# Differential attention scores as three 64-row products per component instead of two stacked 128-row products

## The chip, the cores and the metric

The kernel runs on one core of one Trainium2 chip. The metric is the device time of one launch in microseconds (us), lower is better. A core has TensorE (PE, the matrix products, with weight loads shown as PEld), VectorE (DVE), ScalarE (ACT), GpSimd (POOL) and SyncE (SP, which here only issues transfers). PE reads its operands from SBUF, 128 partitions of on-chip memory, and writes its results to PSUM.

## The reference

The network is an encoder of two layers on 512 tokens with 1024 channels. Each layer projects the normalised input and mixes tokens in three parallel branches (differential attention, a convolution module, neighbourhood attention on an 8 x 64 grid), merges them by gates, and then runs a gated feed-forward part and a gated embedding. The change touches the differential attention alone. It has four heads; each head has two components `c` of 64 channels:

```python
q = apply_rope(q, cos, sin)
k = apply_rope(k, cos, sin)
...
s = jnp.einsum('bhcqd,bhckd->bhcqk', qi, k).astype(f32) * scale
a = jax.nn.softmax(s, axis=-1)
a = (a[:, :, 0] - lam * a[:, :, 1]).astype(v.dtype)
return jnp.einsum('bhqk,bhkd->bhqd', a, v)
```

So for each head and each block of 128 queries there are two score matrices of 128 x 512, each a product over 64 channels; two softmaxes; their difference; and a product with the values. All of it is in float32.

## The kernel before

**Products in halves.** PE multiplies the type float32r, which keeps fewer bits than float32. To keep float32 accuracy each operand is split into a high half (rounded to float32r) and a low half (the rest, again float32r): `split` (L162) makes the high half by an ACT copy and the low half by a DVE subtraction. A general product then is three products into one PSUM tile: high by high, high by low, low by high (`mm3`, L175). The low-by-low term is left out there.

**Order of the work.** The program is written out layer by layer in `layer` (L428). The order of PE's instructions is the order in which the program issues them; the other engines are ordered by a scheduler that follows their dependencies and priorities. While PE works through the projections of one branch, pieces of attention are put in between: `later` (L107) puts a generator in a queue, and every fourth group of three products (`chunk`, L115) one `tick` (L94) may start or go on with one. Each differential head queues four `diff_unit`s (L844), one per block of 128 queries, two ticks apart. A unit runs `probs` (L892), which makes the scores and the softmax difference; every second unit goes on three ticks later with eight transposes (L859) for its pair of blocks and two ticks after that with the product with the values.

**Queries and keys of a head.** `diff_in` (L813) projects queries and keys of one head, each 128 rows (two components of 64) by 512 tokens. It copies the projection out of PSUM into `raw`, makes a rotated copy `rot` with four small transfers (L829), applies the position tables on DVE, and splits the result into `nat` (high, tile tag `kh`) and `low` (in place in `raw`). Then `stack` (L654) copies these halves by transfers of 64 partitions on SP's queue into a layout with one component per column block and the halves above each other: in `st4` (tag `qk`, two buffers) rows 0 to 63 hold a component's high half and rows 64 to 127 its low half; in `k2` (tag `x`, four buffers) the keys stand the other way round, low above high. That is four transfers for the queries and eight for the keys of each head (L660).

**Scores.** `scores` (L807) contracts over all 128 rows at once. The first product, stacked queries by stacked keys, gives high by high plus low by low; the second, stacked queries by the swapped keys, gives high by low plus low by high. So one component costs two products of 128 rows by 512 columns, and both components of a block four. `probs` takes a PSUM tile (tag `sc`, two buffers) for a component, makes its scores, then its maximum on DVE (L902) and its exponential on ACT (L143, a helper's line), and goes on to the other component. The neighbourhood attention uses `stack` and `scores` as well, with its own tiles.

**Who shares the buffers.** The tag `x` also holds the gate accumulators of `gate_c` (L762), which ACT copies out of PSUM. The tags `rp` (four buffers), `kh` (two) and `qk` (two) are also used by other stages.

Of the kernel before, what the change touches and what calls it, by code (L numbers as in the profile page):

```python
# [12 lines left out]
F32R = mybir.dt.float32r  # L13
# [7 lines left out]
P = 128  # L21
# [40 lines left out]
class Net:  # L62
# [744 lines left out]
    def scores(self, out, st4, k2, u, qs, ks):  # L807


        for n, st in enumerate((st4[:, 2 + u], k2[:, u])):  # L810
            self.nc.tensor.matmul(out, st4[:, u, qs], st[:, ks], start=n == 0, stop=n == 1)  # L811

    def diff_in(self, head, st, ys):  # L813
        self.phase = "diff"
        if head == 0:
            st["tabs"] = []
            for t in range(2):
                c = self.sb("r", [P, 512])
                self.nc.sync.dma_start(c, self.a["rope"][t])
                st["tabs"].append(c)  # L820
        st4 = self.sb("qk", [P, 4, 512], F32R)
        k2 = self.sb("x", [P, 2, 512], F32R)
        for s, off in enumerate((OFF_QA, OFF_KA)):
            ps = self.proj(off + head * P)
            raw, rot = self.sb("rp", [P, 512]), self.sb("rp", [P, 512])
            self.act(raw, ps, AF.Copy, scale=1.0 if s else 0.125)
            for b in range(4):
                o = b ^ 1
                self.nc.sync.dma_start(rot[32 * b:32 * b + 32], raw[32 * o:32 * o + 32])  # L829
            self.background(self.tt(raw, raw, st["tabs"][0], ALU.mult), self.bg["diff"])  # L830
            self.tt(rot, rot, st["tabs"][1], ALU.mult)
            self.tt(raw, raw, rot, ALU.add)
            nat, low = self.sb("kh", [P, 512], F32R), raw.bitcast(F32R)
            self.split(nat, low, raw)
            self.stack(nat, low, st4[:, 2 * s:2 * s + 2], k2 if s else None)
        box = dict(s0=self.sb("sm", [P, 4]))
        for qt in range(4):
            self.later(self.diff_unit(head, qt, st4, k2, st, box, ys), 6 if head else 7, 2)

    def diff_v(self, g, st):  # L840
        self.phase = "diff"
        st["v", g] = self.values(self.a["w_va"][self.i, g], lambda v, a: ((v[:, 0:256], v[:, 256:512], a),))

    def diff_unit(self, head, qt, st4, k2, st, box, ys):  # L844

        nc, i = self.nc, self.i
        half, t = qt // 2, qt % 2
        box[qt] = self.probs(st4, k2, qt, box["s0"])
        if t == 0:
            return  # L850
        yield 3
        ats = [box[2 * half], box[2 * half + 1]]
        pps = []
        for kp in range(2):
            pt = self.ps("tr", (P, 2, 256))
            for u in range(2):
                for t in range(2):
                    kc = 2 * kp + u
                    nc.tensor.transpose(pt[:, u, t * P:(t + 1) * P],  # L859
                                        ats[t][:, kc * P:(kc + 1) * P], self.ident)  # L860
            pp = self.sb("pt", [P, 2, 2, 256], F32R)
            self.split(pp[:, 0], pp[:, 1], pt)
            pps.append(pp)
        yield 2
        if half == 0:
            box["av"] = self.ps("av")
        av = box["av"]
        cs = slice((head % 2) * P, (head % 2) * P + P)
        for kp in range(2):
            for u in range(2):  # L870
                v = st["v", head // 2][kp][:, u].rearrange("p (a b) -> p a b", a=2)
                self.mm3(av[:, half * 256:half * 256 + 256], v[:, 0, cs], v[:, 1, cs],
                         pps[kp][:, 0, u], pps[kp][:, 1, u], kp * 2 + u == 0, kp * 2 + u == 3)
        if half == 0:
            return

        eps = self.sb("sm", [P, 4])
        self.stt(eps, box["s0"], EPS, box["s0"], ALU.mult, ALU.mult)
        o = self.sb("t", [P, 512])
        sq = self.sb("ss", [P, 512])  # L880
        self.act(sq, av, AF.Square)
        self.act(o, av, AF.Copy, scale=self.subg[:, i:i + 1])

        def done(col, bc):
            self.tt(o, o, bc, ALU.mult)
            y = self.sb("y", [P, 2, 512], F32R)
            self.split(y[:, 0, :], y[:, 1, :], o)
            ys.append(y)

        yield from self.norm(sq, P, (1, 2), done, spread=False, eps=eps)  # L890

    def probs(self, st4, k2, qt, s0):  # L892


        nc, i = self.nc, self.i
        qs = slice(qt * P, (qt + 1) * P)
        m = self.sb("s", [P, 10])
        es = []
        for u in range(2):
            sc = self.ps("sc")  # L900
            self.scores(sc, st4, k2, u, qs, slice(0, 512))
            nc.vector.tensor_reduce(out=m[:, u:u + 1], in_=sc, op=ALU.max, axis=AX.X, negate=True)  # L902
            e = self.sb("e" if u else "a", [P, 512])
            self.act(e, sc, AF.Exp, table="exp", bias=m[:, u:u + 1],
                     accum_out=m[:, 3:4] if u else s0[:, qt:qt + 1])
            es.append(e)
        nc.vector.reciprocal(m[:, 4:5], m[:, 3:4])
        self.stt(m[:, 5:6], m[:, 4:5], self.nlam[:, i:i + 1], s0[:, qt:qt + 1],
                 ALU.mult, ALU.mult)
        self.stt(es[0], es[1], m[:, 5:6], es[0], ALU.mult, ALU.add)  # L910
        return es[0]
# [555 lines left out]
```

## Time and profile before

| what | us |
|---|---|
| time, median of 3 runs | 1776.03 |
| lowest and highest run | 1776.01, 1777.37 |
| span of the profiled execution, first to last instruction | 1776.7 |
| PE busy in it | 1767.5 |
| DVE busy | 1421.7 |
| ACT busy | 894.4 |

The profiled execution's own device time is not listed apart from its span; the span lies inside the range of the runs. In the profile's lines L12 is line 12 of the kernel, and a tile is named by the stage in which it was made and its tag: `diff_qk` is the stacked tile of the differential attention, `diff_x` its `k2`, `diff_sc` its scores. `out<-in` names what is written and read, `x16` is a count. A duration of PE is that of one product from its start to its modelled end; products are pipelined, so the distance of two starts, and not the duration, is what one costs in a row of them. A view of waits gives the total in us, how many times, and the longest. A form such as `128*128 128x512` gives first the rows and columns of the array that a product is set for, then the size of the result.

### The profile page before, as it was taken

What the parts mean: (1) busy time and instruction counts of PE and PEld (TensorE: products, weight loads), DVE (VectorE), ACT (ScalarE), POOL (GpSimd) and SP (SyncE); (2) the same over time, 40 slices, a digit from 0 to 9 for tenths busy, and PEclk for the clock granted to TensorE, in tenths of its full rate; (3) what the DMA queues carried; (4) which work ended last, traced back from release to release, by engine and by line L of the source; (5) the groups of instructions that cost most, each with busy time, mean ns of one, the idle gap of its engine ahead of it and who ended that gap; (6) DMA issues with size and microseconds to landing.
All of it is one profiled execution on the core that took longest, in us unless ns stands there. A gap on an engine that the chain in (4) does not pass through costs nothing.

```text
span 1776.7 us, 27451 instructions
## 1 busy us (share of the span) xinstructions
PE 1767.5 (99%) x10210; PEld 1559.6 (88%) x10210; DVE 1421.7 (80%) x2418; ACT 894.4 (50%) x1561; POOL 103.0 (6%) x146
## 2 busy tenths in 40 slices
PE   9999999999999999999999999999999999999998
PEld 7888888888899899998888888888888998989987
DVE  7878887998798587787776788889887976867776
ACT  5577555225565254454545765452356643534454
POOL 0000000000111010100000000000001110101000
PEclk9999999999999999999999999999999999999999
DMA  5666641334757366543447655423357664655332
GB/s 202 188 186 176 161 125 42 113 98 140 230 150 193 109 167 160 132 131 123 145 124 198 176 165 149 113 71 95 93 179 198 171 179 115 173 144 151 98 108 92
DMA packets 113509, 256.07 MB, mean 144 GB/s; under 512 B 14560, under 2 KB 19424, under 8 KB 113376
## 3 DMA queue, kind: packets, MB, share of 16 engines
q1 hardware_dynamic: 99984, 229.93, 42.3%
q0 software_dynamic: 12672, 23.07, 8.3%
q8 instruction: 81, 1.33, 0.3%
q10 hardware_dynamic: 720, 1.31, 0.2%
q14 instruction: 52, 0.43, 0.1%
HBM read 215.46 MB, written 7.34 MB: 125 GB/s over the span
## 4 chain that ended last, share of the span: by engine, by line
PE 96%; DVE 2%; ACT 1%; issue 0%; DMA 0%; POOL 0%; ACTq 0%; POOLq 0%; DVEq 0%
PE ffn_mm L1017 4%; PE ffn_mm L1019 4%; PE ffn_mm L177 4%; PE ffn_mm L179 4%; PE ffn_mm L178 4%; PE ffn_mm L1018 4%; PE ffn_sc L1019 3%; PE ffn_sc L1017 3%; PE ffn_sc L1018 3%; PE mergea_mm L177 2%; PE mergea_mm L178 2%; PE mergea_mm L179 2%; PE diff_sc L811 2%; PE gatec_mm L177 2%; PE gatec_mm L178 2%; PE gatec_mm L179 2%
## 5 line engine op out<-in xcount | busy, mean ns | idle before, releaser
L160 DVE SCALAR_TENSOR_TENSOR conv_z<-glu_z,pre_par,conv_z 128x512 f32<-128x512 f32 x240 | 179.4, 748 | 3.3
L143 ACT ACTIVATE ffn_wh<-ffn_wr 128x1024 fp32r<-128x1024 f32 (+1 forms) x92 | 92.7, 1014 | 111.7 <-PE ffn_mm L178 77.1
L987 POOL DMA_DIRECT2D ffn_qk<-w_fu x88 | 78.0, 990 | 605.7 <-DMA ffn_qk<-w_fu 414.7
L157 DVE TENSOR_TENSOR ffn_wl<-ffn_wr,ffn_wh 128x1024 fp32r<-128x1024 f32 (+1 forms) x92 | 107.4, 1173 | 5.4 <-ACT ffn_wh L143 4.9
L157 DVE TENSOR_TENSOR ffn_t<-ffn_mm,wo_rb 128x512 f32<-128x512 f32 (+1 forms) x64 | 38.6, 604 | 67.9 <-PE ffn_mm L179 67.8
L143 ACT ACTIVATE mergea_wh<-mergea_wr 128x1024 fp32r<-128x1024 f32 (+1 forms) x32 | 27.1, 846 | 96.8 <-PE mergea_mm L178 79.6
L143 ACT ACTIVATE ffn_wh<-ffn_qk 128x1024 fp32r<-128x1024 f32 x44 | 46.7, 1060 | 35.9 <-PE ffn_mm L178 15.7
L157 DVE TENSOR_TENSOR ffn_wl<-ffn_qk,ffn_wh 128x1024 fp32r<-128x1024 f32 x44 | 53.8, 1224 | 11.3 <-ACT ffn_wh L143 11.3
L157 DVE TENSOR_TENSOR ffn_t<-ffn_t,ffn_t 128x512 f32<-128x512 f32 (+1 forms) x46 | 31.3, 680 | 31.4 <-ACT ffn_t L143 30.9
L143 ACT ACTIVATE diff_a<-diff_sc,diff_s 128x512 f32<-128x512 f32 x32 | 22.0, 686 | 61.0 <-DVE diff_s L902 61.0
L177 PE MATMUL ffn_mm<-ffn_v,ffn_wh 128*128 128x512 f32 x132 | 51.4, 389 | 0.0
L178 PE MATMUL ffn_mm<-ffn_v,ffn_wh 128*128 128x512 f32 x132 | 51.4, 389 | 0.0
L179 PE MATMUL ffn_mm<-ffn_v,ffn_wl 128*128 128x512 f32 x132 | 51.3, 389 | 0.0
L177 PE MATMUL ffn_mm<-ffn_y,ffn_wh 128*128 128x512 f32 x132 | 51.3, 389 | 0.0
L178 PE MATMUL ffn_mm<-ffn_y,ffn_wh 128*128 128x512 f32 x132 | 51.3, 389 | 0.0
L179 PE MATMUL ffn_mm<-ffn_y,ffn_wl 128*128 128x512 f32 x132 | 51.3, 389 | 0.0
L1019 PE MATMUL ffn_mm<-wo_h,ffn_wl 128*128 128x256 f32 x176 | 49.8, 283 | 0.0
L1019 PE MATMUL ffn_sc<-wo_h,ffn_wl 128*128 128x256 f32 x176 | 49.8, 283 | 0.0
L1018 PE MATMUL ffn_mm<-wo_h,ffn_wh 128*128 128x256 f32 x176 | 49.8, 283 | 0.0
L1018 PE MATMUL ffn_sc<-wo_h,ffn_wh 128*128 128x256 f32 x176 | 49.8, 283 | 0.0
L1017 PE MATMUL ffn_sc<-wo_h,ffn_wh 128*128 128x256 f32 x176 | 49.8, 283 | 0.0
L1017 PE MATMUL ffn_mm<-wo_h,ffn_wh 128*128 128x256 f32 x176 | 49.8, 283 | 0.0
(876 smaller groups left out, 6588.6 us busy)
## 6 DMA issues: line engine op xcount, KB each, us to landing
ffn_qk<-w_fu POOLq DMA_DIRECT2D x88, 256.0 KB, 5.7
ffn_wr<-w_fg SPq DMA_DIRECT2D x44, 512.0 KB, 3.7
ffn_wr<-w_fd SPq DMA_DIRECT2D x32, 448.0 KB, 3.9
ffn_r<-w_fu SPq DMA_DIRECT2D x44, 256.0 KB, 3.7
ffn_qk<-w_fg SPq DMA_DIRECT2D x44, 256.0 KB, 4.3
ffn_qk<-w_fu SPq DMA_DIRECT2D x44, 256.0 KB, 4.6
natten_wr<-w_in SPq DMA_DIRECT2D x16, 512.0 KB, 4.3
natten_b<-bias SPq DMA_DIRECT2D x32, 256.0 KB, 4.0
```

Source lines behind the costliest of these rows:

```text
L143: i = self.nc.scalar.activation(out, in_, func, **kw)
L157: return self.nc.vector.tensor_tensor(out, a, b, op)
L160: return self.nc.vector.scalar_tensor_tensor(out, a, s, b, op0, op1)
L177: mm(out, wh, ah, start=first, stop=False)
L178: mm(out, wh, al, start=False, stop=False)
L179: mm(out, wl, ah, start=False, stop=last)
L811: self.nc.tensor.matmul(out, st4[:, u, qs], st[:, ks], start=n == 0, stop=n == 1)
L987: nc.gpsimd.dma_start(q, wu[:, lo], accum_op=ALU.add)
L1017: mm(out, wh[:, c], bh, start=first and k == 0, stop=False, skip_group_check=True)
L1018: mm(out, wh[:, c], bl, start=False, stop=False, skip_group_check=True)
L1019: mm(out, wl[:, c], bh, start=False, stop=k == 3, skip_group_check=True)
```

## The change

The stacked tile and `k2` go. `diff_in` splits queries and keys straight into `st4`, whose four column blocks now hold queries high, queries low, keys high, keys low, with component 0 in rows 0 to 63 and component 1 in rows 64 to 127, as the projection leaves them. `stack` is no longer called for this branch, and its transfers are not issued. `probs` takes both PSUM tiles first and calls the new `both_scores`, which makes three products of 64 rows for each component (high by high, high by low, low by high), the two components in turn. The low-by-low term is left out now, as in the kernel's other products. Maximum, exponential and all that follows are as before, but come after all six products in the program.

```diff
+    def both_scores(self, outs, st4, qs, ks):
+
+        for n, (a, b) in enumerate(((0, 2), (0, 3), (1, 2))):
+            for u, out in enumerate(outs):
+                r = slice(64 * u, 64 * u + 64)
+                self.nc.tensor.matmul(out, st4[r, a, qs], st4[r, b, ks], start=n == 0, stop=n == 2)
...
         st4 = self.sb("qk", [P, 4, 512], F32R)
-        k2 = self.sb("x", [P, 2, 512], F32R)
...
             self.tt(raw, raw, rot, ALU.add)
-            nat, low = self.sb("kh", [P, 512], F32R), raw.bitcast(F32R)
-            self.split(nat, low, raw)
-            self.stack(nat, low, st4[:, 2 * s:2 * s + 2], k2 if s else None)
+            self.split(st4[:, 2 * s], st4[:, 2 * s + 1], raw)
...
-        for u in range(2):
-            sc = self.ps("sc")
-            self.scores(sc, st4, k2, u, qs, slice(0, 512))
+        scs = [self.ps("sc") for _ in range(2)]
+        self.both_scores(scs, st4, qs, slice(0, 512))
+        for u, sc in enumerate(scs):
             nc.vector.tensor_reduce(out=m[:, u:u + 1], in_=sc, op=ALU.max, axis=AX.X, negate=True)
```

The remaining lines of the diff only drop the argument `k2` from `diff_unit` and `probs`.

More of the change, by code (lines that the diff above doesn't have):

```diff
@@ L832, in diff_in @@
             self.tt(raw, raw, rot, ALU.add)
-            nat, low = self.sb("kh", [P, 512], F32R), raw.bitcast(F32R)
-            self.split(nat, low, raw)
-            self.stack(nat, low, st4[:, 2 * s:2 * s + 2], k2 if s else None)
+            self.split(st4[:, 2 * s], st4[:, 2 * s + 1], raw)
         box = dict(s0=self.sb("sm", [P, 4]))
         for qt in range(4):
-            self.later(self.diff_unit(head, qt, st4, k2, st, box, ys), 6 if head else 7, 2)
+            self.later(self.diff_unit(head, qt, st4, st, box, ys), 6 if head else 7, 2)
     def diff_v(self, g, st):
@@ L842, in diff_v, with diff_unit @@
         st["v", g] = self.values(self.a["w_va"][self.i, g], lambda v, a: ((v[:, 0:256], v[:, 256:512], a),))
-    def diff_unit(self, head, qt, st4, k2, st, box, ys):
+    def diff_unit(self, head, qt, st4, st, box, ys):
         nc, i = self.nc, self.i
         half, t = qt // 2, qt % 2
-        box[qt] = self.probs(st4, k2, qt, box["s0"])
+        box[qt] = self.probs(st4, qt, box["s0"])
         if t == 0:
@@ L890, in diff_unit, with probs @@
         yield from self.norm(sq, P, (1, 2), done, spread=False, eps=eps)
-    def probs(self, st4, k2, qt, s0):
+    def probs(self, st4, qt, s0):
         nc, i = self.nc, self.i
```

## The prediction

> **What bounds the kernel now.** I read the page's first and fourth parts, then the waits of TensorE, then busy time by stage, and last the score products one by one.
>
> ```profile
> span 1776.7 us, 27451 instructions
> PE 1767.5 (99%) x10210; PEld 1559.6 (88%) x10210; DVE 1421.7 (80%) x2418; ACT 894.4 (50%) x1561; POOL 103.0 (6%) x146
> ...
> PE 96%; DVE 2%; ACT 1%; issue 0%; DMA 0%; POOL 0%; ACTq 0%; POOLq 0%; DVEq 0%
> ```
>
> TensorE (PE) is busy for all but 9.2 us and holds 96% of the chain that ended last. That share alone does not say that every stage is bound by it; the next view does (columns: length, then busy time and count of PE, weight loads, DVE, ACT, POOL, granted clock, DMA share, GB/s). Differential attention runs from 152 to 300 us in layer 0 and from 1032 to 1180 in layer 1.
>
> ```profile
> 152.00:174.00 22.00, 21.61 (x140) 19.05 (x139) 17.52 (x46) 16.92 (x44) 0.30 (x2) 1.00 0.65 171
> 174.00:300.00 126.00, 126.00 (x689) 108.61 (x688) 104.53 (x185) 69.39 (x141) 3.03 (x3) 1.00 0.41 110
> ...
> 1032.00:1054.00 22.00, 21.58 (x137) 18.93 (x137) 17.98 (x47) 16.42 (x44) 0.30 (x2) 1.00 0.62 168
> 1054.00:1180.00 126.00, 126.00 (x689) 108.61 (x688) 104.53 (x185) 69.82 (x142) 3.02 (x3) 1.00 0.39 109
> ```
>
> PE is busy for 126.00 of 126.00 us in both layers, at a granted clock of 1.00. The only holes are 0.39 and 0.42 us in the hand-over from neighbourhood attention. So nothing that merely arrives earlier can pay more than about 0.8 us; only a different cost on PE moves the end. The score products on PE (start, duration; a group is four products, two components):
>
> ```profile
> 172.56 0.93 PE diff_sc L811 x4
> ...
> 1167.21 0.93 PE diff_sc L811 x4
> ```
>
> These are the first and the last of 32 such pieces in the chain of waits (2 layers, 4 heads, 4 query tiles). They lie between 0.91 and 0.99 us; I use 0.93, so 32 x 0.93 = 29.8 us. One group in the timeline of PE:
>
> ```profile
> 201.48 0.28 PE L619 MATMUL diff_mm<-diff_wh,glu_h 128*128 128x256 f32 x1
> 201.60 0.40 PE L811 MATMUL diff_sc<-diff_qk 128*128 128x512 f32 x1
> 201.83 0.40 PE L811 MATMUL diff_sc<-diff_x,diff_qk 128*128 128x512 f32 x1
> 202.07 0.39 PE L811 MATMUL diff_sc<-diff_qk 128*128 128x512 f32 x1
> 202.30 0.40 PE L811 MATMUL diff_sc<-diff_x,diff_qk 128*128 128x512 f32 x1
> 202.53 0.28 PE L615 MATMUL diff_mm<-diff_wh,glu_h 128*128 128x256 f32 x1
> ```
>
> Two numbers matter. A 512-column product starts 0.23 us after the one before it, yet lasts 0.39 us: neighbours overlap by 0.16 us, as the end of one passes through the array while the next streams in. And every product is of the form 128*128: the trace has no product on 64 rows.
>
> **The change: PE.** Each group goes from four products on 128 rows to six on 64 rows, rows 0 to 63 and 64 to 127 in turn, into two PSUM tiles. Three prices are unknown.
>
> First, *does a product on one half run beside one on the other?* The nearest rows are the products above, which never share the array: by them six cost 6 x 0.23 = 1.38 us. If pairs run fully side by side they cost 3 x 0.23 = 0.69 us.
>
> Second, *the weights.* Each product loads its own. What a load costs when the product is too short to hide it is seen in the transposes:
>
> ```profile
> 189.82 0.39 PE L179 MATMUL diff_mm<-glu_h,diff_wl 128*128 128x512 f32 x1
> 190.05 1.03 PE L859 MATMUL diff_tr<-pre_ident,diff_a 128*128 128x128 f32 x8
> 190.84 0.48 PE L177 MATMUL diff_mm<-glu_h,diff_wh 128*128 128x512 f32 x1
> 191.16 0.40 PE L178 MATMUL diff_mm<-glu_h,diff_wh 128*128 128x512 f32 x1
> ```
>
> Eight take 1.03 us with the last one's own 0.27 us (272 ns, median of this line), so they start (1.03 - 0.27) / 7 = 0.11 us apart for a quarter of the columns. If loads come one after another at 0.11 us, the two halves start 0.11 us apart: the sixth product starts at 2 x 0.23 + 0.11 = 0.57 us, and the next full-height product can follow 0.23 us later, so a group costs 0.80 us. I take 0.80 for an overlapping group, between 0.69 and, with nothing shared, 1.38.
>
> ```profile
> L859 PE MATMUL diff_tr<-pre_ident,diff_a x128: 270/272/273, 190.1 to 1178.4; 128*128 128x128 f32 x128
> ```
>
> Third, *the switch between full-height and half-height products*, twice per group. The rows above show another switch, to transposes and back: 190.05 comes 0.23 us after 189.82, so that switch costs nothing. But transposes keep the form 128*128. If the array must run empty before its rows are regrouped, the overlap of 0.39 - 0.23 = 0.16 us is lost each time. If the weights for the other form can't be loaded ahead either, part of a load shows too: behind the transposes the second product starts 0.32 us after the first instead of 0.23, which is 0.09 us of load laid bare; at most it is a whole load:
>
> ```profile
> L811 PEld LDWEIGHTS diff_sc<-diff_qk x64: 187/188/192, 172.3 to 1167.3; 128*128 128x128 f32 x64
> L811 PE MATMUL diff_sc<-diff_qk x64: 389/396/478, 172.3 to 1167.5; 128*128 128x512 f32 x64
> ```
>
> So a switch is worth 0 to 0.16 + 0.19 = 0.35 us; I take 0.16 + 0.09 = 0.25, twice 0.50. It is no measured price: no row has a change of height, and I take the middle since the two overlaps that such a change could break are both there to be lost.
>
> The Trainium skill, "TensorEngine Tiling (Array Packing)", Key Properties, states that tiles on different rows load weights and multiply in parallel, and also that changing the tiling mode, not just the tile, drains the TensorE. The first alone would make this change faster; the second speaks against it, 64 times over. No run here shows either.
>
> Sum for the forecast: 0.80 + 0.50 = 1.30 us a group against 0.93, so +0.37 x 32 = **+11.8 us**.
>
> **The change: transfers.** The stacking copies go:
>
> ```profile
> diff_qk<-diff_kh SPq DMA_DIRECT2D x32, 128.0 KB, 2.3
> diff_qk<-diff_rp SPq DMA_DIRECT2D x32, 128.0 KB, 2.3
> ...
> diff_x<-diff_kh SPq DMA_DIRECT2D x16, 128.0 KB, 2.3
> diff_x<-diff_rp SPq DMA_DIRECT2D x16, 128.0 KB, 3.1
> ```
>
> That is 96 copies of 128 KB, 12.6 MB, and SP's waits for them:
>
> ```profile
> SPq L660 <- ACT diff_kh L143: 32.7, 12, 5.2
> ```
>
> Weight loads queued behind on SP go out up to 5.2 us earlier, and the tiles of k2 and of the stacked halves come free. I count all of it at 0: PE has no idle time there, save the 0.8 us in the hand-over, which wait for ACT and DVE and not for a transfer:
>
> ```profile
> PE natten_tr L734 <- ACT natten_e L143: 0.3, 2, 0.2
> PE natten_tr L736 <- ACT natten_e L143: 0.3, 2, 0.2
> PE natten_tr L736 <- DVE natten_a L157: 0.2, 1, 0.2
> ```
>
> **The change: new waits.** ACT's copy and DVE's subtraction stay, with the same shapes, but write the qk tile directly, so ACT now waits for one of its two buffers, where before SP did. Behind a waiting ACT stand the exponentials and weight splits. Head 2's copy needs head 0's last score, head 3's needs head 1's:
>
> ```profile
> 194.34 0.39 PE L811 MATMUL diff_sc<-diff_x,diff_qk 128*128 128x512 f32 x1
> ...
> 207.56 0.63 ACT L143 ACTIVATE diff_kh<-diff_rp 128x512 fp32r<-128x512 f32 x1
> ...
> 226.01 0.39 PE L811 MATMUL diff_sc<-diff_x,diff_qk 128*128 128x512 f32 x1
> ...
> 233.95 0.63 ACT L143 ACTIVATE diff_kh<-diff_rp 128x512 fp32r<-128x512 f32 x1 [3.45 <-issue]
> ```
>
> Both are free by 12.8 and 7.5 us: 0. The second component's PSUM tile is written 0.3 to 0.4 us sooner in the group than now. Its last reader ends at 216.15 and the next group starts at 217.47:
>
> ```profile
> 215.94 0.21 ACT L143 ACTIVATION_READ_ACCUMULATOR diff_e<-diff_sc,diff_s 128x1 f32 x1
> 217.47 0.48 PE L811 MATMUL diff_sc<-diff_qk 128*128 128x512 f32 x1
> ```
>
> 1.3 us to spare, so 0; without it PE itself would stall, 32 times at most some tenths. The first component's maximum is taken 0.1 to 0.8 us later; its transposes come only after the next group, 6 us on.
>
> **The forecast.** The span of 1776.7 us lies within 0.7 us of the median of 1776.03, so the difference is put on the median: 1776.0 + 11.8 = **1787.8 us**. With the bounds of this case, 0.69 + 0.32 = 1.01 and 0.80 + 0.70 = 1.50 us a group: 1778.6 to 1794.3.
>
> **The rivals.**
>
> *Overlap, and switching is free* (ends on the other side). 0.80 us a group: -0.13 x 32 = -4.2, 1771.9 us; with 0.69, -7.7, 1768.3 us; I write 1770. It decides wherever the two switches together cost under 0.13 us. For it: transposes switch at no cost. Against it: transposes leave the height as it is.
>
> *No overlap.* 1.38 us: +0.45 x 32 = +14.4, 1790.4 us. For it: in this trace a product's pace goes by its columns, and no two share the array. Against it: nothing here had the chance to.
>
> *Neither overlap nor a free switch.* 1.38 + 0.50: +30.4, 1806 us.
>
> *It does nothing:* if 0.80 and switches of 0.06 cancel, time stands still. That lies between the first two cases.
>
> **Chances.** Forecast 0.36, free switching 0.34, no overlap 0.22, neither 0.06, something else 0.02. Under 0.2%, 3.6 us, a measurement of this kernel can't be told from no change. Of free switching 0.28 lies below 1772.5 us; the forecast's cheap end gives the rest of "same": faster 0.29, same 0.12, slower 0.59. The range runs from 1768.5, the full overlap, to 1796.0, past the forecast's dear end; it leaves out "neither" and the tails. The slower cases alone: 1778.6 to 1796.0. Free switching is nearly as likely as the forecast, and since those two have opposite signs I hold the sign only weakly.
>
> **What would show it.** Six rows of 64 rows a group in PE's timeline. Overlap: starts 0.11 apart in pairs, 0.23 between products of one half; none: 0.23 throughout. Switch: the gap before the first and behind the last of a group, against 0.23. The chain's pieces for the scores should be 1.30 us (0.80 or 1.38 by the rivals), and PE still busy throughout 174 to 300 us. I am wrong in kind if idle time appears on PE there, or if the pace of other products moves from 0.23.

## The result, and the profile after

| | before | after |
|---|---|---|
| time, median, us | 1776.70 | 1790.82 |
| lowest and highest | 1776.01, 1778.10 | 1789.95, 1791.05 |
| span of the profiled execution | 1776.7 | 1788.2 |
| its own time | not listed | 1789.95 |

The change makes the kernel slower: the ratio is 1.0079, with a 95% interval from 1.0064 to 1.0093, or +14.1 us. The time lies 1.75 us above the span after. By the same step the profiled execution of before would have taken about 1778.4 us, somewhat more than its median, so the two spans (11.5 us apart) understate the difference. Effects of whole kernels are given below by medians.

First the page after: span, busy time by engine, the chain by engine.

```profile
span 1788.2 us, 27420 instructions
PE 1775.3 (99%) x10274; PEld 1552.7 (87%) x10274; DVE 1424.0 (80%) x2418; ACT 897.9 (50%) x1561; POOL 103.2 (6%) x146
...
PE 93%; DVE 3%; ACT 2%; issue 1%; DMA 1%; SPq 0%; POOL 0%; POOLq 0%; DVEq 0%; ACTq 0%
```

PE is still busy 99% of the time, but its share of the chain fell from 96 to 93% and DVE's rose from 2 to 3%: some of the new time is spent waiting for DVE. Busy time by stage says where (columns as in the prediction):

```profile
152.00:174.00 22.00, 19.49 (x128) 17.34 (x127) 16.50 (x43) 16.00 (x42) 0.30 (x2) 1.00 0.26 77
174.00:307.00 133.00, 132.95 (x738) 107.41 (x739) 109.11 (x191) 72.01 (x145) 3.04 (x3) 1.00 0.25 75
```

In differential attention proper, from 174 us, PE is idle for 0.05 us in layer 0 and, from 1054 us, 0.43 us in layer 1; before, both stretches had none. The hand-over from neighbourhood attention lost: 19.49 us busy of 22, where it was 21.61 (in layer 1 19.62, where it was 21.58). The view of PE's waits names it:

```profile
PE natten_sc L811 <- DVE natten_s L710: 4.8, 4, 1.9
```

This row is new. PE waits 4.8 us in all, twice in each layer, for DVE's maxima of the last neighbourhood scores (L710), to get their PSUM tile back.

**The products.** One group of scores in PE's timeline, after, and below it the same place before:

```profile
196.30 0.39 PE L179 MATMUL diff_mm<-glu_h,diff_wl 128*128 128x512 f32 x1
196.62 0.97 PE L818 MATMUL diff_sc<-diff_qk 64*128 64x512 f32 x6
197.52 0.50 PE L177 MATMUL diff_mm<-glu_h,diff_wh 128*128 128x512 f32 x1
197.85 0.40 PE L178 MATMUL diff_mm<-glu_h,diff_wh 128*128 128x512 f32 x1
```

```profile
193.44 0.39 PE L179 MATMUL diff_mm<-glu_h,diff_wl 128*128 128x512 f32 x1
193.66 0.39 PE L811 MATMUL diff_sc<-diff_qk 128*128 128x512 f32 x1
...
194.79 0.39 PE L178 MATMUL diff_mm<-glu_h,diff_wh 128*128 128x512 f32 x1
```

A group is best priced from a full-height product ahead of it to the second one behind it, less two normal steps of 0.23 us, since what a switch breaks shows only on the second. After: 1.55 - 0.46 = 1.09 us. Before: 1.35 - 0.46 = 0.89 us. That is +0.20 us for this group, which is among the dearest: between products of 256 columns the same distance is 1.32 us after and 1.17 us before. Added up from the starts of all 32 groups, the products cost 5.5 us more. In the records the two products of a pair start at most 15 ns apart, so the halves do run side by side: three pairs of 0.23 us are 0.69 us, and 0.40 us is left for two switches. After each switch the first product (or pair) comes 0.32 instead of 0.23 us behind its predecessor, and the second 0.33 us behind the first. The weight loads of a pair run side by side as well:

```profile
196.62 0.19 PEld L818 LDWEIGHTS diff_sc<-diff_qk 64*128 64x128 f32 x2 [0.35 <-ACT diff_rp L143]
```

Two loads of 0.18 us each have both ended 0.19 us after the first began.

**The order on DVE.** DVE's timeline at the hand-over, before and after:

```profile
152.53 0.42 DVE L710 CUSTOM_DVE_ANT_0 natten_b<-natten_sc,natten_b 128x256 f32<-128x256 f32 x1 [0.73 <-PE natten_sc L811]
...
152.88 1.22 DVE L157 TENSOR_TENSOR diff_wl<-diff_wr,diff_wh 128x1024 fp32r<-128x1024 f32 x1
```

```profile
152.25 0.68 DVE L157 TENSOR_TENSOR diff_rp<-diff_rp,diff_r 128x512 f32<-128x512 f32 x1
152.85 1.22 DVE L157 TENSOR_TENSOR diff_wl<-diff_wr,diff_wh 128x1024 fp32r<-128x1024 f32 x1
153.99 0.74 DVE L160 SCALAR_TENSOR_TENSOR conv_z<-glu_z,pre_par,conv_z 128x512 f32<-128x512 f32 x1
154.65 0.68 DVE L157 TENSOR_TENSOR diff_rp<-diff_rp,diff_r 128x512 f32<-128x512 f32 x1
...
155.82 0.69 DVE L157 TENSOR_TENSOR diff_rp<-diff_rp,diff_rp 128x512 f32<-128x512 f32 x1
...
156.99 0.42 DVE L710 CUSTOM_DVE_ANT_0 natten_b<-natten_sc,natten_b 128x256 f32<-128x256 f32 x1
```

Before, DVE waited 0.73 us for the neighbourhood scores and took their maximum as soon as they stood. After, the scheduler has put a weight split, a step of the convolution and a head's position work (`diff_rp`, three instructions) ahead of it. The maximum starts at 156.99 instead of 152.53, and PE stands still.

**The clock.** PE's timeline has these waits in both layers, and only in the second does the pace of PE change behind them:

```profile
157.48 0.39 PE L811 MATMUL natten_sc<-natten_qk 128*128 128x256 f32 x1 [1.93 <-DVE natten_s L710]
...
158.43 0.39 PE L811 MATMUL natten_sc<-natten_qk 128*128 128x256 f32 x1 [0.44 <-DVE natten_s L710]
...
1042.48 0.39 PE L811 MATMUL natten_sc<-natten_qk 128*128 128x256 f32 x1 [1.93 <-DVE natten_s L710]
...
1043.43 0.39 PE L811 MATMUL natten_sc<-natten_qk 128*128 128x256 f32 x1 [0.44 <-DVE natten_s L710]
...
1044.60 0.42 PE L615 MATMUL diff_mm<-diff_wh,ple_h 128*128 128x256 f32 x1
1044.82 0.41 PE L617 MATMUL diff_mm<-diff_wl,ple_h 128*128 128x256 f32 x1
```

```profile
1044.00:1048.00 4.00, 4.00 (x23) 4.00 (x22) 0.82 (x5) 2.50 (x9) 0.00 (x0) 0.57 0.46 123
```

Products of 256 columns that otherwise start 0.12 us apart start 0.22 us apart here, at a granted clock of 0.57 over 4 us. The clock missing is 0.43 x 4 = 1.7 us; at half rate that is a stretch of 3.4 us. So waits of 2.4 us were followed here by a further loss of 1.7 us.

Four terms can be read from the profiled executions: 5.5 us in the products, 4.1 us more idle time at the two hand-overs (2.12 and 1.96), 0.5 us of it behind them, and 1.7 us of clock. That is 11.8 us, against 11.5 us between the two spans.

### The profile page after: what moved, and what is told of

It is laid out like the page before. It is cut to its first block, busy times and chain, and to the rows that moved or that the text cites. A ratio compares the mean times of both kernels' runs of the same rounds, so it can differ in the third digit from the quotient of the medians.

```text
span 1788.2 us, 27420 instructions
## 1 busy us (share of the span) xinstructions
PE 1775.3 (99%) x10274; PEld 1552.7 (87%) x10274; DVE 1424.0 (80%) x2418; ACT 897.9 (50%) x1561; POOL 103.2 (6%) x146
## 4 chain that ended last, share of the span: by engine, by line
PE 93%; DVE 3%; ACT 2%; issue 1%; DMA 1%; SPq 0%; POOL 0%; POOLq 0%; DVEq 0%; ACTq 0%
PE ffn_mm L1021 4%; PE ffn_mm L1023 4%; PE ffn_mm L177 4%; PE ffn_mm L178 4%; PE ffn_mm L179 4%; PE ffn_mm L1022 4%; PE ffn_sc L1023 3%; PE ffn_sc L1021 3%; PE ffn_sc L1022 3%; PE mergea_mm L177 2%; PE mergea_mm L179 2%; PE mergea_mm L178 2%; PE gatec_mm L177 2%; PE gateb_mm L177 2%; PE gateb_mm L178 2%; PE gateb_mm L179 2%
```

## The experiments

Two theories stood against each other after the result. *Theory:* about +6 us come from the products (halves run side by side, switches cost 0.2 us each), and the rest comes from the hand-over, through DVE's order and the half-rate clock. *Rival:* it is all in the products, as the prediction had it; the total of +14.1 us is close to the +14.4 us of "no overlap". Times of before are 1776.55 to 1776.80 us in the three groups of runs.

**scores_only: the products alone.** The products on 64 rows as in the change; the halves still go through the tiles `kh` and `k2` by transfers of 128 KB, in number and size as before.

```diff
...
-            self.split(st4[:, 2 * s], st4[:, 2 * s + 1], raw)
+            nat, low = self.sb("kh", [P, 512], F32R), raw.bitcast(F32R)
+            self.split(nat, low, raw)
+            self.place(nat, low, st4[:, 2 * s:2 * s + 2], k2 if s else None)
```

> The changed products alone: twelve transfers per head stay, in number, size and place, but lay the halves into the unstacked layout, so the three 64-row products per component read what they read in the changed kernel. Theory: the change costs twice, once by the products (a group takes 3 x 0.23 + 2 switches of 0.20 = 1.09 us instead of 0.90, +0.19 x 32 = +6 us) and once by a stall at the hand-over from neighbourhood attention (2 to 3 us a layer, +5 us), which comes from DVE taking the key's position work ahead of the neighbourhood scores' maxima once the transfers no longer hold it back. With the transfers DVE's order is the one of before, so this kernel is +6 us, 1782 to 1784, and PE idles less than 1 us from 152 to 175 us. Rival (the six products do not overlap and the records only look so): +14 us, 1790, as the changed kernel.

Measured: 1783.12 us, ratio 1.0036 (1.0023 to 1.0048), +6.3 us. In its timeline of PE a group stands between the same products:

```profile
193.87 0.39 PE L179 MATMUL diff_mm<-glu_h,diff_wl 128*128 128x512 f32 x1
194.19 0.50 PE L819 MATMUL diff_sc<-diff_qk 64*128 64x512 f32 x2
...
195.42 0.40 PE L178 MATMUL diff_mm<-glu_h,diff_wh 128*128 128x512 f32 x1
```

Again 1.55 us from the first to the last, so 1.09 us a group. PE has no wait at `natten_sc`, and DVE takes the maximum when it did before:

```profile
152.44 0.42 DVE L710 CUSTOM_DVE_ANT_0 natten_b<-natten_sc,natten_b 128x256 f32<-128x256 f32 x1 [0.73 <-PE natten_sc L811]
```

The products are worth +6.3 us (4.1 to 8.5 by the interval; the starts gave 5.5); the rival falls, since they don't carry the whole.

**transfers_only: the transfers alone.** Four products on 128 rows a group, as before, but on the unstacked tile, with no transfers, no `k2` and no `kh` tile. The scores are then not the reference's: each contracts over both components.

```diff
-        for n, (a, b) in enumerate(((0, 2), (0, 3), (1, 2))):
-            for u, out in enumerate(outs):
-                r = slice(64 * u, 64 * u + 64)
-                self.nc.tensor.matmul(out, st4[r, a, qs], st4[r, b, ks], start=n == 0, stop=n == 2)
+        for u, out in enumerate(outs):
+            for n in range(2):
+                self.nc.tensor.matmul(out, st4[:, u, qs], st4[:, 2 + n, ks], start=n == 0, stop=n == 1)
```

> The removed transfers alone: queries and keys stay unstacked without transfers, and each group makes four products of 128 rows as before. Such a product runs over both components at once, so the scores are not the reference's; only the time is of use. Theory: PE's work per group is that of before (0.90 to 0.93 us), DVE's order is that of the changed kernel, so the hand-over stalls alone are left: +5 us, 1780 to 1783. Rival (the removed transfers are worth nothing and all the loss lies in the products): 1776 to 1777.

Measured: 1785.81 us, ratio 1.0051 (1.0038 to 1.0064), +9.0 us: more than expected. The largest wait of PE, and two stretches of 4 us:

```profile
PE natten_sc L811 <- DVE natten_s L710: 5.3, 4, 2.4
```

```profile
160.00:164.00 4.00, 4.00 (x25) 4.00 (x25) 0.59 (x2) 2.48 (x8) 0.15 (x1) 0.65 0.46 131
...
1044.00:1048.00 4.00, 4.00 (x25) 4.00 (x25) 0.59 (x2) 2.30 (x7) 0.00 (x0) 0.64 0.45 131
```

The expectation had the wait but not the clock, which dips in both layers here. Its trace accounts for the loss: against before, PE is idle 4.4 us longer at the two hand-overs and 1.6 us longer behind them, and the clock, granted at 0.92 over each hand-over of 22 us, costs 3.5 us: 9.5 us in all. Taking the transfers, with their tiles, away costs time where PE's work is as before, so a saving that the prediction counted at 0 is a loss. The two parts alone add up to 6.3 + 9.0 = 15.3 us, against 14.1 for the whole change; the intervals are wide enough for that, and the change's trace has one stretch at half rate where this one has two.

**pinned: the change, with the maxima moved forward.** The last maxima of neighbourhood attention get a higher priority with the scheduler.

```diff
-            nc.vector.tensor_tensor_reduce(
+            with self.tc.high_priority(offset=150 if pr == 3 else 0):
+                nc.vector.tensor_tensor_reduce(
...
```

> The changed kernel with one thing more: the maximum (with bias) of the last neighbourhood heads' scores gets a higher scheduling priority, so that DVE takes it ahead of the key's position work again. Theory: the stall at the hand-over goes at least in part, 2 to 5 us below the changed kernel: 1785 to 1788. Rival (no stall of DVE's making): as the changed kernel, 1790.

Measured: 1784.73 us, ratio 1.0045 (1.0033 to 1.0058), 6.1 us below the change. DVE's maximum, PE's largest wait at the hand-over, and the stretch of 4 us in layer 1 in which the clock dipped:

```profile
154.51 0.42 DVE L711 CUSTOM_DVE_ANT_0 natten_b<-natten_sc,natten_b 128x256 f32<-128x256 f32 x1
```

```profile
PE natten_tr L737 <- ACT natten_e L143: 1.4, 2, 1.0
```

```profile
1044.00:1048.00 4.00, 3.99 (x23) 3.46 (x24) 2.97 (x8) 3.90 (x11) 0.15 (x1) 1.00 0.28 83
```

The maximum starts 2.5 us earlier than in the change, though still 2 us later than before. The wait at `natten_sc` is gone, a smaller one in the transposes behind it heads the list, and the granted clock is 1.00 instead of 0.57. So the order on DVE is the cause of these 6.1 us, and not something the transfers did for PE directly. The repair is not whole: PE waits 2.8 us at these transposes, where before it waited 0.8, and the kernel stays 1.6 us behind scores_only, which keeps the transfers.

**transfers_pinned: transfers_only with the same priority.** The scores are again not the reference's.

> The removed transfers alone (four products of 128 rows on unstacked tiles, so the scores are not the reference's), with the higher priority for the last neighbourhood heads' maxima as well. Theory (the removed transfers cost time only through DVE's order at the hand-over, and through the half-rate clock that the idle time brings on): most of the +9 us of the removed transfers goes, 1777 to 1780, and the granted clock has no dip. Rival (the loss comes from elsewhere, such as the copies that now write the tile directly): 1784 to 1787.

Measured: 1779.95 us, ratio 1.0018 (1.0010 to 1.0027). Of the +9.0 us, +3.2 are left; PE waits 3.3 us at transposes, where before it waited 0.8. DVE takes the maximum at 154.67, behind one `diff_rp` and the weight split:

```profile
154.67 0.43 DVE L711 CUSTOM_DVE_ANT_0 natten_b<-natten_sc,natten_b 128x256 f32<-128x256 f32 x1
```

This holds with the products as they were, so the repair doesn't depend on the 64-row form.

**in_sequence: three products of one component, then three of the other.** If two neighbours in the program must lie on different halves to run side by side, this loses the overlap.

```diff
-        for n, (a, b) in enumerate(((0, 2), (0, 3), (1, 2))):
-            for u, out in enumerate(outs):
+        for u, out in enumerate(outs):
+            for n, (a, b) in enumerate(((0, 2), (0, 3), (1, 2))):
```

> The changed kernel with the order of the six products changed: the three of one component, then the three of the other, instead of in turn. Theory (products on different halves run side by side, products on one half follow each other at 0.23 us): at most the third and the fourth can share the array, so a group takes 5 or 6 x 0.23 + 0.40 = 1.55 to 1.78 us instead of 1.09, +15 to +22 us above the changed kernel: 1805 to 1813. Rival (nothing overlaps): the same time as the changed kernel, 1790.

Measured: 1790.58 us, ratio 1.0079 (1.0064 to 1.0094): no different from the change, and the expectation failed. Its timeline of PE:

```profile
197.55 0.39 PE L179 MATMUL diff_mm<-glu_h,diff_wl 128*128 128x512 f32 x1
197.87 0.97 PE L818 MATMUL diff_sc<-diff_qk 64*128 64x512 f32 x6
198.77 0.50 PE L177 MATMUL diff_mm<-glu_h,diff_wh 128*128 128x512 f32 x1
```

Six products still take 0.97 us and begin in pairs, the second of a pair now some 10 ns behind the first, where it was 1 to 5 ns in most pairs of the change. The records don't name the component of a product. Either each half works through its own products in order, whatever stands between them in the program (new theory), or any two 64-row products overlap, on whichever half (new rival).

**one_half: all six products on rows 0 to 63.** The second component's scores are then those of the first. This tells the two apart.

```diff
-                r = slice(64 * u, 64 * u + 64)
+                r = slice(0, 64)
```

> The changed kernel with all six products of a group on rows 0 to 63, so that both components are computed from component 0 (the output is not the reference's). The order of the six did not matter in the run before; two readings are left. Theory (each half takes its own products in its own order, beside the other half): six on one half follow each other, 6 x 0.23 + 0.40 = 1.76 us a group instead of 1.09, +21 us over the changed kernel, 1809 to 1814, and the starts in the records are single, 0.23 us apart. Rival (any two neighbouring products of 64 rows go in one slot, or a product of 64 rows is simply twice as fast): the same time as the changed kernel, 1790.

Measured: 1811.74 us, ratio 1.0199 (1.0185 to 1.0213), 20.9 us above the change.

```profile
191.14 0.39 PE L179 MATMUL diff_mm<-glu_h,diff_wl 128*128 128x512 f32 x1
191.46 1.66 PE L818 MATMUL diff_sc<-diff_qk 64*128 64x512 f32 x6
193.04 0.50 PE L177 MATMUL diff_mm<-glu_h,diff_wh 128*128 128x512 f32 x1
```

Six products now take 1.66 us, 0.69 more, and 32 x 0.69 = 22 us. The new rival falls, and with it the chance that a 64-row product is simply cheaper. This is also what "no overlap" with paid switches costs, and it is far from the change's time.

**dummy_full and dummy_half: the switch by itself.** The kernel before with one extra product a group, ahead of the first component's two, overwritten by them: on 128 rows in the one, on 64 in the other. Their difference is two switches.

```diff
             sc = self.ps("sc")
+            if u == 0:
+                nc.tensor.matmul(sc, st4[:, 0, qs], st4[:, 2, 0:512], start=True, stop=True)
```

The second has `0:64` in place of the first index of both operands.

> The kernel before with one more product of 128 rows and 512 columns ahead of each of the 32 score groups, into the tile that the first true product then overwrites. It is the control for the next run. Every theory: 32 x 0.23 = +7.3 us over the kernel before, 1783 to 1785.

> The kernel before with one more product of 64 rows (rows 0 to 63) and 512 columns ahead of each score group, overwritten by the first true product. Theory (a switch between full and half height costs about 0.20 us, whatever follows): 0.23 + 2 x 0.20 = 0.63 us a group, +20 us over the kernel before, 1795 to 1799, and 11 to 15 us over the control. Rival (a switch is free, and what the groups of the changed kernel lose lies in their six loads): +7.3 us, as the control.

Measured: 1783.76 us (ratio 1.0041, 1.0027 to 1.0055) and 1795.95 us (1.0110, 1.0096 to 1.0123): +7.2 and +19.4 us. The first is 7.2 / 32 = 0.23 us a product, the pace in the trace. The difference of 12.2 us is 0.38 us a group, 0.19 us a switch. In the timeline of dummy_half:

```profile
203.76 0.28 PE L619 MATMUL diff_mm<-diff_wh,glu_h 128*128 128x256 f32 x1
203.97 0.49 PE L902 MATMUL diff_sc<-diff_qk 64*128 64x512 f32 x1
204.39 0.50 PE L811 MATMUL diff_sc<-diff_qk 128*128 128x512 f32 x1
204.72 0.40 PE L811 MATMUL diff_sc<-diff_x,diff_qk 128*128 128x512 f32 x1
```

The 64-row product starts 0.21 us after one of 256 columns (0.12 otherwise), the next 0.42 us later (0.23 otherwise), the one behind it 0.33 us later: 0.09 + 0.19 + 0.10 = 0.38 us.

**pair and pair_by_block: two blocks a switch.** If the switch decides, half as many switches should win. Two blocks of queries make their twelve products together, the second block's scores in two PSUM tiles of the transposes (tag `tr`); the transfers are kept. The first kernel takes the blocks in turn, the second one block after the other.

```diff
-        for qt in range(4):
-            self.later(self.diff_unit(head, qt, st4, st, box, ys), 6 if head else 7, 2)
+        for qt in (1, 3):
+            self.later(self.diff_unit(head, qt, (st4, k2), st, box, ys), 6 if head else 7, 4)
...
+        pairs = [[self.ps(tag) for _ in range(2)] for tag in ("sc", "tr")]
+        self.both_scores(pairs, st4, [slice(b * P, (b + 1) * P) for b in (qt - 1, qt)], slice(0, 512))
...
```

> The changed products with the transfers kept, as in the first run, but two query blocks at a time: twelve products of 64 rows in a row, into the two score tiles and the two transpose tiles, so a switch to half height and back is paid 16 times instead of 32. Theory (0.23 us per pair of products plus 0.40 us per group for the switches): 6 x 0.23 + 0.40 = 1.78 us per two blocks against 2 x 1.09, -0.40 x 16 = -6.4 us against the run with the transfers kept (1783.1), so 1776 to 1779, about the kernel before. A stall would show as idle time of PE at the transposes, as four maxima and exponentials must be done before the transpose tiles are free. Rival (the groups lose by their loads and not by the switches): 1783.

> The run with two blocks at a time, with one change: the twelve products go block by block, the six into the score tiles first and the six into the transpose tiles behind them, so the transpose tiles are needed 0.69 us later in the group. In the run before PE waited 7.0 us, 14 times, for these tiles, 0.2 to 1.0 us each, in the middle of a group. Theory (the switches are paid once for two blocks, 1.79 us per two blocks as its records show, and the run lost by those waits alone): most of the waits vanish, 1777 to 1781. Rival (two blocks at a time lose by something else, or the switch is not what a group loses): 1788 to 1791 as before.

Measured: 1790.73 us (ratio 1.0080, 1.0067 to 1.0094) and 1786.41 us (1.0056, 1.0042 to 1.0070). The first expectation failed; the second lies between its two theories. PE's timeline, then waits, of pair:

```profile
188.32 0.39 PE L179 MATMUL diff_mm<-glu_h,diff_wl 128*128 128x512 f32 x1
188.64 0.50 PE L820 MATMUL diff_sc<-diff_qk 64*128 64x512 f32 x2
...
190.57 0.39 PE L178 MATMUL diff_mm<-glu_h,diff_wh 128*128 128x512 f32 x1
```

```profile
PE diff_tr L820 <- DVE diff_pt L157: 2.7, 4, 0.7
PE diff_tr L820 <- DVE diff_t L157: 2.2, 4, 1.0
```

Without a wait, two blocks cost 2.25 - 0.46 = 1.79 us, as much as two groups of before (2 x 0.89 = 1.78), so this form had nothing to win; and it pays for the borrowed tiles, which DVE is still reading. In pair_by_block the same price is paid for a group without a wait, and these waits add up to 3.7 us, against 6.9 us in pair. A group with two of them:

```profile
235.68 0.39 PE L179 MATMUL gatec_mm<-glu_h,gatec_wl 128*128 128x512 f32 x1
...
237.15 0.50 PE L820 MATMUL diff_tr<-diff_qk 64*128 64x512 f32 x1 [0.19 <-DVE diff_pt L157]
238.35 0.50 PE L820 MATMUL diff_tr<-diff_qk 64*128 64x512 f32 x1 [0.70 <-DVE diff_pt L157]
...
239.58 0.40 PE L178 MATMUL gatec_mm<-glu_h,gatec_wh 128*128 128x512 f32 x1
```

From the product ahead to the second one behind this takes 3.90 us, where a group without a wait takes 2.25. So 1.65 us are lost, though the listed waits are only 0.19 + 0.70 = 0.89 us: a listed wait counts only the time in which no product runs, and here the two products of a pair also start 1.20 us apart instead of together. By an estimate from the starts of all 16 groups, against groups without a wait, pair_by_block loses 8.0 us in this way. With 1.3 us of waits at the transposes that were not there before, this places nearly all of its +9.6 us. No form that was tried beats the kernel before.

## Why the prediction was right, and where it was not

The direction and the range held, and the forecast, 1787.8 us, was 3.0 us short. The range took in faster times as well as slower ones, so that it held says little, and the direction was held only weakly (0.59 for slower). The sum came near by luck, through two errors that nearly cancel: it had +11.8 us from products and 0 from transfers, where the parts measured alone give +6.3 and +9.0 us.

- **"0.80 for an overlapping group"**: 0.69. The step that failed is "loads come one after another at 0.11 us": weight loads of the two halves run side by side too (two in 0.19 us), and both products of a pair start within 15 ns rather than 0.11 us apart. The Trainium skill, "TensorEngine Tiling (Array Packing)", Key Properties, states that tiles load and multiply in parallel; the trace agrees.
- **"I take 0.16 + 0.09 = 0.25" for a switch**: 0.19 to 0.20 us. Both gaps that it added up are there, but as 0.09 us ahead of the first product and 0.10 us ahead of the second, so the first term, a whole overlap of 0.16 us, was too dear. The Trainium skill's drain on a change of tiling mode, in the same section, agrees in that a change has a price; whether the array runs empty the modelled ends can't show.
- So the group shown costs 1.09 us, not 1.30, against 0.89 and not 0.93 before: +0.20, not +0.37. The chain's pieces of 0.9 us that the prediction named as a sign would have misled: a piece starts at the first 64-row product and leaves out 0.09 us before it and 0.10 us behind it.
- **Transfers, "I count all of it at 0"**: +9.0 us, the step that failed worst. The reason given was that PE had no idle time there. That shows only that earlier data can't *help*; it says nothing of what a released dependency lets the scheduler do. Without the transfers a head's position work came sooner on DVE, ahead of a maximum for which PE came to wait 1.93 us; with them, in scores_only, DVE kept its order. pinned and transfers_pinned show the order to be the main cause. By which dependency the scheduler came to that order is argued and not shown: which of the removed parts (the transfers, `kh`, or the buffers of tag `x`) let the scheduler do so was not tried apart.
- **New waits at 0**: right. PE's waits name no `diff_sc`, and PE, busy for 132.95 of 133.00 us in layer 0 and 132.57 in layer 1, was hardly held up there, so no wait of ACT's for the `qk` buffer reached it.
- **"Idle time on PE from 174 to 300"** as the sign of an error in kind: there was 0.05 us. The idle time came some 15 us earlier, in the hand-over whose 0.8 us the prediction had itself quoted as the only hole.
- **Free switching** fell with the dummies. **No overlap** gave 1790.4 us, nearest to the measured time, and is wrong: one_half, without the overlap, is 20.9 us slower. A total can't choose between mechanisms.

## What to carry to other kernels

Row halves of the array do run side by side, so short contractions can share it, but each change between full and half height cost 0.2 us, close to a whole 512-column product: gather the half-height work, and count switches before products. When a change takes dependencies away, list what becomes free on each engine that is ordered by priorities, and look for an instruction behind which the busiest engine waits; an unchanged count of instructions is no proof of an unchanged order. Moving that one instruction forward gave back 6 us here, both with the changed products and with the old ones; but with the changed products, keeping the transfers was 1.6 us better still (1783.12 against 1784.73 us), so measure both. And read the loss by a wait from the starts of the products around it, not from the listed wait alone.

## What the runs showed of the hardware

- **Each half has its own order.** In in_sequence the fourth product of the program starts beside the first, on the other half, ahead of the second and third; six take 0.97 us as in the change. This rests on the pairs in the records, on one_half, where six on one half take 1.66 us, and on PE getting its products in the program's order, which the trace doesn't show by itself. The Trainium skill, "TensorE: Matmul & The Clock Gate", Part 3: Packing small matmuls — row/col tiling, states that products keep program order at start and end; the measurement differs from that across row halves. On one half they do follow each other, at 0.23 us.
- **Half rate can follow short waits.** Behind waits of 1.93 and 0.44 us the clock cost a further 1.7 us in layer 1 of the profiled execution of the change, and nothing in layer 0, though they were the same. In pair it followed two waits of 0.65 and 0.71 us in layer 1, while the same group in layer 0, with 0.66 and 0.70 us, kept a clock of 1.00:

```profile
1124.00:1128.00 4.00, 3.94 (x14) 2.73 (x15) 2.98 (x6) 1.62 (x6) 0.00 (x0) 0.57 0.64 150
```

The Trainium skill, "TensorE: Matmul & The Clock Gate", Part 1: The HAM clock gate, gives a free-running window of about 3.4 us; the stretch of 3.4 us at half rate agrees, though none of these waits is as long as that, and a window's phase would explain why only one of two equal gaps was hit. No run here sets the phase, so that is argued and not shown.
